# Indexer scores of the first 128 tokens: one matmul over two half-length key runs, added on the way out of PSUM

## The chip, the cores and the metric

One core of a Trainium2 chip runs the whole kernel. The metric is the device time of an execution in microseconds. The matmuls run on TensorE (PE in the profile), elementwise work on VectorE (DVE) and ScalarE (ACT), a few masks on GpSimd (POOL); SyncE (SP) issues the DMAs.

## The reference

A decoder trunk of two layers over 256 tokens of width 1024. In each layer a normed input is projected to eleven parts. Branch A is attention over the 64 keys that an indexer picks for each query; branch B is a gated linear recurrence; both are gated, merged and projected back. What the change touches is the indexer:

```
dots = einsum('bqhd,bsd->bqhs', iq, ik)          # 16 heads of 64, one key vector per position
idx_score = einsum('bqh,bqhs->bqs', iw, relu(dots))
idx_score = where(key_pos <= query_pos, idx_score, -inf)
sel = top_k(idx_score, 64)
```

Because of the causal mask, a query among the first 128 tokens needs the scores of the first 128 keys only.

## The kernel before

Activations stand transposed in SBUF, 128 features by 256 tokens. Every float32 operand of a matmul is split into a high part, rounded to the fast float32 format of TensorE (`F32R`), and a low part, the remainder; a product is the sum of three matmuls (high x high, low x high, high x low; function `mm3`). The weights stream from HBM in chunks of 128x1024 (`raw`), which ScalarE or VectorE rounds to `wh` and VectorE subtracts to `wl`; a chunk feeds 8 blocks, so 24 matmuls of 256 columns, or fewer of 512.

The program is not written in the order in which it runs. `Program` records every operation with an engine, a cost and its tiles. `issue` then plans: it takes, over all engines, the operation that can start first, and among those that can start at once the one that is due first. A TensorE operation is due at its place in the written order plus `pg.late`; `LATE_DOTS` puts the dots 40 us of matmul time later than they are written, so that they are spread between other matmuls. The other engines' operations are due when a matmul needs them or a buffer of a ring must be free again (`deadlines`). Each engine then runs its list strictly in that order. So a change of one function moves instructions in the whole program.

The indexer, class `Layer`: `head` makes the keys (`ikr`, 64x256), writes the rounded half `kh` and the rest `kl` twice, on partitions 0 to 63 and 64 to 127. `queries` turns two pairs of heads into `st`, two tiles that hold one head's high and low part one above the other on the 128 partitions, so that one matmul with `kh` gives high x high and low x high, and one with `kl` the rest. `dots` then runs for 8 pairs of heads and for `t` = 0 and 1, the first and the last 128 tokens. It takes one of two PSUM banks of the pool `pq` (which also serves the gate matmuls `gps` and the attention logits `lg`), makes four matmuls of 256 columns into it, takes the Relu on ScalarE into `rl`, and adds both heads, weighted, to the scores `wk` on VectorE. For `t` = 0 all 256 keys are multiplied, and 128 are read:

```
            for a in range(2):
                w = st[a][:, t * P:t * P + P]
                mm(ps[:, a, :], w, self.kh, True, False)
                mm(ps[:, a, :], w, self.kl, False, True)
            ...
            act(rl[:, :, :n], ps[:, :, :n], AF.Relu)
```

In the profile's rows `dots` is the bank, `iqs` are the tiles `st`, `rps` the matmuls of the recurrent branch, `mb`, `ma` and `ga` gates, `xc` the convolution, `sg` an activated gate, `g` its split product. Helpers record the operations, so their lines stand in the rows: L506 ScalarE, L513 and L515 the rounding copy on ScalarE or VectorE, L519 VectorE with two tensors, L534 and L538 VectorE with a scalar, L545 matmul, L548 transpose, L552 and L1031 DMAs.

Of the kernel before, what the change touches and what calls it, by code (L numbers as in the profile page):

```python
# [12 lines left out]
F32R = mybir.dt.float32r  # L13
I32 = mybir.dt.int32
AF = mybir.ActivationFunctionType
OP = mybir.AluOpType

P = 128
D = 1024
T = 256  # L20
# [221 lines left out]
def real(a):  # L242
    return a.ap() if isinstance(a, V) else a
# [222 lines left out]
def trunk(ctx, tc, xT, pos, pre, par, fgb, wst, out):  # L466
# [7 lines left out]
    pg = Program()  # L474
    cnt = [0]

    def nm(s):
        cnt[0] += 1
        return f"{s}{cnt[0]}"


    def const(s, shape, dt=F32, bufs=1, tag=None):
        return pg.tile(cp, tag or s, [P] + shape, dt, nm(s), bufs)
# [7 lines left out]
    def f2(s):  # L491
        return pg.tile(fp, "f2", [P, 2, T], F32, nm(s), F2)
# [4 lines left out]
    def bank(pool, s):  # L497
        return pg.tile(pp, pool, [P, 2, T], F32, nm(s), {"pp": 4, "pq": 2, "pt": 2}[pool])


    def act(o, i, func, **kw):
        c = (160 if i.psum() else 140) + 0.833 * o.size() + (200 if "accum_out" in kw else 0)
        aps = [kw[k] for k in ("scale", "bias") if isinstance(kw.get(k), V)]
        outs = [o] + ([kw["accum_out"]] if "accum_out" in kw else [])
        pg.op("act", c + 93 * len(aps), outs, [i] + aps,
              lambda: nc.scalar.activation(real(o), real(i), func, **{k: real(v) for k, v in kw.items()}),  # L506
              TABS.get(func))
# [9 lines left out]
    def tt(op, o, a, b):  # L517
        pg.op("dve", 67 + 1.046 * o.size(), [o], [a, b],
              lambda: nc.vector.tensor_tensor(real(o), real(a), real(b), op=op))  # L519
# [4 lines left out]
    def add(o, a, b):  # L524
        tt(OP.add, o, a, b)
# [4 lines left out]
    def tsc(o, a, s1, s2, op0, op1=None):  # L530
        c = 67 + 1.046 * o.size() if a.psum() else 69 + 0.52 * o.size()
        kw = {} if op1 is None else {"op1": op1}
        pg.op("dve", c, [o], [a, s1, s2],
              lambda: nc.vector.tensor_scalar(real(o), real(a), real(s1), real(s2), op0=op0, **kw))  # L534

    def stt(o, a, s, b, op0, op1):
        pg.op("dve", 129 + 1.046 * o.size(), [o], [a, s, b],
              lambda: nc.vector.scalar_tensor_tensor(real(o), real(a), real(s), real(b), op0=op0, op1=op1))  # L538
# [4 lines left out]
    def mm(o, w, m, start, stop, grp=False, cost=None):  # L543
        pg.op("pe", cost or (m.size() + 32) / 2.4, [o], [w, m],
              lambda: nc.tensor.matmul(real(o), real(w), real(m), start=start, stop=stop, skip_group_check=grp))  # L545
# [15 lines left out]
    class Stream:  # L561
        def __init__(self):
            self.pos = 0
            self.raws = {}
            self.parts = {}
            self.nload = 0
# [257 lines left out]
    class Layer:  # L824
        def __init__(self, l, xg, norm):
            self.l = l
            self.xg = xg
            self.norm = norm
            self.h = []
            self.sga, self.sma, self.smb = {}, {}, {}  # L830
            self.xc, self.xs, self.rix, self.sy, self.g = {}, {}, {}, {}, {}
            self.rope = {}
            self.aT = []
            self.m = []
            self.banks = {}
            self.wk = [const("wk0", [P]), const("wk1", [T])]
            self.kh = const("kh", [T], F32R)
            self.kl = const("kl", [T], F32R)
            self.iwq = const("iwq", [2, 16])

        def pair(self, key, i):
# [69 lines left out]
        def dots(self, i, st, t):  # L911

            pg.late = LATE_DOTS
            ps = bank("pq", "dots")
            for a in range(2):
                w = st[a][:, t * P:t * P + P]
                mm(ps[:, a, :], w, self.kh, True, False)
                mm(ps[:, a, :], w, self.kl, False, True)
            pg.late = 0.0
            n = P * (t + 1)  # L920
            o = self.wk[t]
            rl = f2("rl")
            act(rl[:, :, :n], ps[:, :, :n], AF.Relu)
            for a in range(2):
                w = self.iwq[:, t, 2 * i + a:2 * i + a + 1]
                if i == 0 and a == 0:
                    tsc(o, rl[:, a, :n], w, None, OP.mult)
                else:
                    stt(o, rl[:, a, :n], w, o, OP.mult, OP.add)
# [444 lines left out]
```

## Time and profile before

| | |
|---|---|
| median of 3 runs | 699.63 us (699.3 to 701.31) |
| the profiled execution | 699.13 us |
| its span, first to last instruction | 697.3 us |
| instructions in the span | 12505 |
| PE busy, matmuls | 686.9 us, 99%, 4684 |
| DVE busy | 601.4 us, 86%, 1177 |
| ACT busy | 480.0 us, 69%, 775 |
| POOL busy | 7.1 us, 1%, 18 |
| HBM read | 119.77 MB |

Busy times are sums over an engine's instructions; a row in the listings below gives the length of one record, and records of one engine overlap at their ends, so the distance from one start to the next is shorter than a record. The chain that ended last is the profile's way of following the end back to what it waited for.

### The profile page before, as it was taken

The page shows a single profiled execution, that of the slowest core. Times are in us where ns is not written, and L with a number is a line of the kernel's source. Part 1 is how long each engine was busy: PE and PEld are TensorE (multiplying, and loading weights), DVE is VectorE, ACT ScalarE, POOL GpSimd, SP SyncE. Part 2 cuts the span into 40 slices and gives each one's busy share as a digit, 9 for nine tenths or more (in the row PEclk, how much of TensorE's full clock was granted, in tenths as well). Part 3 has the DMA queues.
Part 4 walks back from the last instruction along what each step waited for, and adds up shares of the span by engine and source line. Part 5 has one row for each costly group of instructions (what it writes and reads, how often), then busy time and mean ns, then how long its engine had stood idle before and what let it go on. Part 6 is the DMA issues. An engine that isn't in the chain of part 4 may idle for free.

```text
span 697.3 us, 12505 instructions
## 1 busy us (share of the span) xinstructions
PE 686.9 (99%) x4684; PEld 636.6 (91%) x4684; DVE 601.4 (86%) x1177; ACT 480.0 (69%) x775; POOL 7.1 (1%) x18
## 2 busy tenths in 40 slices
PE   9999999999999999999999999999999999999996
PEld 8988999998899998888999999999999898988885
DVE  7999999999898959857779999989978987897563
ACT  7898675698996748534559766688879765664433
POOL 0000000000000000000000000000000000000000
PEclk9999999999999999999999999999999999999998
DMA  8745666776756462665553566766675655445621
GB/s 281 238 153 166 211 187 195 218 206 200 212 180 200 152 189 65 209 182 183 170 176 118 185 192 184 198 211 197 222 207 185 186 184 156 147 145 161 197 72 61
DMA packets 37697, 125.24 MB, mean 180 GB/s; under 512 B 4677, under 2 KB 6661, under 8 KB 37637
## 3 DMA queue, kind: packets, MB, share of 16 engines
q1 hardware_dynamic: 37636, 124.44, 57.9%
q8 instruction: 37, 0.61, 0.4%
q14 instruction: 24, 0.19, 0.1%
HBM read 119.77 MB, written 1.05 MB: 173 GB/s over the span
## 4 chain that ended last, share of the span: by engine, by line
PE 87%; DVE 2%; ACT 1%; DMA 0%; issue 0%
PE rps L545 15%; PE yb L545 9%; PE q L545 7%; PE k L545 7%; PE ops L545 6%; PE ya L545 6%; PE v L545 6%; PE mb L545 6%; PE ga L545 6%; PE ma L545 5%; PE gps L545 4%; PE iq L545 3%; PE dots L545 2%; PE av L545 2%; PE lg L545 2%; PE ptp L548 1%
## 5 line engine op out<-in xcount | busy, mean ns | idle before, releaser
L519 DVE TENSOR_TENSOR wl<-raw,wh 128x1024 fp32r<-128x1024 f32 x223 | 271.3, 1220 | 57.7 <-ACT wh L513 56.1
L513 ACT ACTIVATE wh<-raw 128x1024 fp32r<-128x1024 f32 x196 | 207.1, 1059 | 136.0 <-PE ya L545 22.4
L545 PE MATMUL rps<-hl,wh 128*128 128x256 f32 x352 | 99.6, 283 | 0.5 <-DVE hl L519 0.5
L545 PE MATMUL rps<-hh,wh 128*128 128x256 f32 x352 | 99.6, 283 | 0.3 <-ACT hh L513 0.3
L545 PE MATMUL rps<-hh,wl 128*128 128x256 f32 x352 | 99.5, 283 | 0.0
L545 PEld LDWEIGHTS rps<-hl,wh 128*128 128x128 f32 x352 | 67.4, 191 | 0.7 <-DVE hl L519 0.7
L545 PEld LDWEIGHTS rps<-hh,wh 128*128 128x128 f32 x352 | 67.3, 191 | 0.7 <-ACT hh L513 0.5
L545 PEld LDWEIGHTS rps<-hh,wl 128*128 128x128 f32 x352 | 67.4, 191 | 0.2
L545 PE MATMUL yb<-wh,g 128*128 128x512 f32 x176 | 59.5, 399 | 0.0
L545 PE MATMUL iq<-xg,wh 128*128 128x256 f32 x232 | 44.9, 285 | 0.0
L545 PE MATMUL ya<-wh,aT 128*128 128x512 f32 x128 | 40.9, 395 | 0.0
L545 PEld LDWEIGHTS yb<-wh,g 128*128 128x128 f32 x176 | 32.4, 188 | 5.5
L545 PEld LDWEIGHTS iq<-xg,wh 128*128 128x128 f32 x232 | 37.2, 192 | 0.0
L545 PE MATMUL ga<-hh,wh 128*128 128x256 f32 x128 | 36.3, 283 | 0.5 <-DVE iqr L519 0.5
L545 PE MATMUL q<-hl,wh 128*128 128x256 f32 x128 | 36.4, 284 | 0.0
L545 PE MATMUL q<-hh,wh 128*128 128x256 f32 x128 | 36.3, 283 | 0.0
L545 PE MATMUL k<-hh,wl 128*128 128x256 f32 x128 | 36.3, 283 | 0.0
L545 PE MATMUL k<-hh,wh 128*128 128x256 f32 x128 | 36.2, 283 | 0.0
L545 PE MATMUL ga<-hl,wh 128*128 128x256 f32 x128 | 36.2, 283 | 0.0
L545 PE MATMUL q<-hh,wl 128*128 128x256 f32 x128 | 36.2, 283 | 0.0
L545 PE MATMUL ga<-hh,wl 128*128 128x256 f32 x128 | 36.2, 283 | 0.0
L545 PE MATMUL k<-hl,wh 128*128 128x256 f32 x128 | 36.2, 283 | 0.0
(269 smaller groups left out, 1923.1 us busy)
## 6 DMA issues: line engine op xcount, KB each, us to landing
raw<-in_wst_dram SPq DMA_DIRECT2D x224, 512.0 KB
xk<-xs SPq DMA_DIRECT2D x24, 48.0 KB
out_dram<-z SPq DMA_DIRECT2D x4, 256.0 KB
xf<-xs SPq DMA_DIRECT2D x8, 80.0 KB
rah<-in_wst_dram SPq DMA_DIRECT2D x2, 256.0 KB
xr<-in_xT_dram SPq DMA_DIRECT2D x1, 512.0 KB
xf<-xs SPq DMA_DIRECT2D x4, 128.0 KB
fg<-in_fgb_dram SPq DMA_DIRECT2D x2, 256.0 KB
```

The source lines that it names most:

```text
L513: lambda: nc.scalar.activation(real(o), real(i), AF.Copy),
L519: lambda: nc.vector.tensor_tensor(real(o), real(a), real(b), op=op))
L545: lambda: nc.tensor.matmul(real(o), real(w), real(m), start=start, stop=stop, skip_group_check=grp))
L548: pg.op("pe", 70, [o], [i, ident], lambda: nc.tensor.transpose(real(o), real(i), real(ident)))
```

## The change

`kh` and `kl` become two halves of one tile `khl`, 128 x 2 x 256. For the first 128 tokens each head gets one matmul whose moving operand is the first 128 columns of both halves, one run after the other: 256 columns, high sums in the first half of the output, low sums in the second. ScalarE copies the low halves of both heads out of the bank, VectorE adds the high halves from the bank, ScalarE takes the Relu in place. For the last 128 tokens the code is what it was.

```
-            self.kh = const("kh", [T], F32R)
-            self.kl = const("kl", [T], F32R)
+            self.khl = const("khl", [2, T], F32R)
+            self.kh, self.kl = self.khl[:, 0, :], self.khl[:, 1, :]
...
             ps = bank("pq", "dots")
-            for a in range(2):
-                w = st[a][:, t * P:t * P + P]
-                mm(ps[:, a, :], w, self.kh, True, False)
-                mm(ps[:, a, :], w, self.kl, False, True)
-            pg.late = 0.0
             n = P * (t + 1)
+            rl = f2("rl")
             o = self.wk[t]
-            rl = f2("rl")
-            act(rl[:, :, :n], ps[:, :, :n], AF.Relu)
+            if t == 0:
+
+                for a in range(2):
+                    mm(ps[:, a, :], st[a][:, :P], self.khl[:, :, :P], True, True)
+                pg.late = 0.0
+                act(rl[:, :, :P], ps[:, :, P:], AF.Copy)
+                add(rl[:, :, :P], rl[:, :, :P], ps[:, :, :P])
+                act(rl[:, :, :P], rl[:, :, :P], AF.Relu)
+            else:
+                for a in range(2):
+                    w = st[a][:, t * P:t * P + P]
+                    mm(ps[:, a, :], w, self.kh, True, False)
+                    mm(ps[:, a, :], w, self.kl, False, True)
+                pg.late = 0.0
+                act(rl, ps, AF.Relu)
```

The order of the instructions, at the two places that the prediction speaks of. In layer 0 on TensorE, a group of dots for the first 128 tokens stood among the matmuls of the recurrent branch like this:

```order
L545 MATMUL dots_897<-kh_762,iqs_665 128x256
L545 MATMUL rps_835<-hl_573,wh_696 128x256
L545 MATMUL dots_897<-kl_791,iqs_665 128x256
L545 MATMUL rps_835<-hh_438,wh_735 128x256
L545 MATMUL dots_897<-kh_762,iqs_672 128x256
L545 MATMUL rps_835<-hh_438,wl_813 128x256
L545 MATMUL dots_897<-kl_791,iqs_672 128x256
```

And with the change, two such groups in the same layer with one for the last tokens:

```order
L545 MATMUL dots_891<-khl_808,iqs_536 128x256
L545 MATMUL dots_891<-khl_808,iqs_544 128x256
L545 MATMUL rps_822<-hh_463,wh_734 128x256
L545 MATMUL rps_822<-hh_463,wl_783 128x256
L545 MATMUL rps_822<-hl_530,wh_734 128x256
L545 MATMUL rps_822<-hh_477,wh_734 128x256
L545 MATMUL rps_822<-hh_477,wl_783 128x256
L545 MATMUL rps_822<-hl_546,wh_734 128x256
L545 MATMUL dots_907<-khl_808,iqs_536 128x256 x2
L545 MATMUL dots_907<-khl_808,iqs_544 128x256 x2
```

A group for the first tokens has two matmuls in place of four, both with the whole key tile, and the groups now stand in blocks between stretches of other matmuls.

In layer 1 on VectorE, before, where the keys' low half is made and the first scores (`wk`) follow:

```order
L519 TENSOR_TENSOR kl_4953<-ikr_4866,kh_4922 64x256
L519 TENSOR_TENSOR sg_4938<-sg_4938,rps_4750 128x256
L519 TENSOR_TENSOR kl_4953<-ikr_4866,kh_4922 64x256
L519 TENSOR_TENSOR ga_4907<-ga_4907,ga_4830 128x512
L519 TENSOR_TENSOR wl_4978<-raw_4815,wh_4889 128x1024
L519 TENSOR_TENSOR wl_4990<-raw_4860,wh_4945 128x1024
L538 SCALAR_TENSOR_TENSOR xc_4986<-rps_4904,prm_213,xc_4986 128x255
L519 TENSOR_TENSOR wl_5010<-raw_4914,wh_4969 128x1024
L534 TENSOR_SCALAR wk_5026<-rl_5006,iwq_4606 128x128
```

With the change, the same place:

```order
L519 TENSOR_TENSOR khl_4957<-ikr_4920,khl_4957 64x256
L519 TENSOR_TENSOR wl_4985<-raw_4859,wh_4937 128x1024
L519 TENSOR_TENSOR khl_4957<-ikr_4920,khl_4957 64x256
L538 SCALAR_TENSOR_TENSOR xc_4987<-rps_4903,prm_213,xc_4987 128x255
L519 TENSOR_TENSOR wl_5004<-raw_4889,wh_4969 128x1024
L538 SCALAR_TENSOR_TENSOR xc_4987<-rps_4903,prm_213,xc_4987 128x254
L519 TENSOR_TENSOR wl_5023<-raw_4946,wh_5000 128x1024
L519 TENSOR_TENSOR rl_5017<-rl_5017,dots_5009 128x2x128
L534 TENSOR_SCALAR wk_5044<-rl_5031,iwq_4605 128x256
```

The keys' subtractions moved behind two weight subtractions (one more stands just ahead of these rows), and the first new addition stands behind two further ones, ahead of the first score. In layer 0 the rows between the last key subtraction and the first addition are of the same kinds and number. Over the whole program the order has 16 additions more on VectorE; on ScalarE 16 Relus more; of the rounding copies, VectorE has 4 more of `g`, one more of `xs`, one less of `wh` and two less of the keys, and ScalarE the opposite; TensorE has 32 matmuls less; SP has the same 305 DMAs.

## Rows read from the trace of the kernel before

**Rows 1.** The page, its parts 1 (busy us, share of the span) and 4 (chain).

```profile
PE 686.9 (99%) x4684; PEld 636.6 (91%) x4684; DVE 601.4 (86%) x1177; ACT 480.0 (69%) x775; POOL 7.1 (1%) x18
...
PE 87%; DVE 2%; ACT 1%; DMA 0%; issue 0%
```

**Rows 2.** Waits of TensorE: releaser, us in total, times, longest; 8 lines.

```profile
PE warm L545 <- DVE hpi L555: 1.1, 1, 1.1
PE dots L545 <- ACT rl L506: 0.5, 1, 0.5
...
PE mb L545 <- DVE ga L519: 0.4, 1, 0.4
...
PE gps L545 <- DMA xf<-xs: 0.2, 1, 0.2
```

**Rows 3.** Stretches: us, then busy of PE, PEld, DVE, ACT, POOL; clock, DMA.

```profile
55.00:70.00 15.00, 14.11 (x99) 12.77 (x99) 14.87 (x29) 13.05 (x24) 0.00 (x0) 1.00 0.64 191
70.00:90.00 20.00, 20.00 (x143) 18.82 (x142) 19.91 (x43) 13.66 (x24) 0.00 (x0) 1.00 0.62 188
...
120.00:150.00 30.00, 30.00 (x231) 29.02 (x230) 28.09 (x70) 22.40 (x38) 0.87 (x2) 1.00 0.70 209
...
395.00:410.00 15.00, 15.00 (x108) 13.87 (x107) 14.94 (x30) 10.65 (x19) 0.00 (x0) 1.00 0.67 210
410.00:428.00 18.00, 18.00 (x126) 16.67 (x125) 17.73 (x38) 11.55 (x21) 0.42 (x1) 1.00 0.58 172
```

**Rows 4.** The chain that ended last: start us, us, instructions.

```profile
119.47 5.76 PE rps L545 x48
125.22 2.75 PE mb L545 x12
...
403.40 0.12 PE dots L545
```

**Rows 5.** Tile dots: instructions, record ns (min/median/max), first and last start, forms.

```profile
L545 PE MATMUL dots<-kh,iqs x64: 277/282/387, 55.3 to 426.0; 128*128 128x256 f32 x64
...
L545 PE MATMUL dots<-kl,iqs x64: 277/284/287, 57.5 to 426.4; 128*128 128x256 f32 x64
L506 ACT ACTIVATE rl<-dots x32: 363/482/604, 58.6 to 426.7; 128x256 f32<-128x256 f32 x16, 128x512 f32<-128x512 f32 x16
```

**Rows 6.** Groups by line and form: busy us, mean ns, idle time before.

```profile
L519 DVE TENSOR_TENSOR sg<-sg,rps 128x256 f32<-128x256 f32 x22 | 9.0, 414 | 0.4 <-ACT sg L506 0.4
...
L506 ACT ACTIVATE asq<-rix 128x256 f32<-128x256 f32 x22 | 8.1, 410 | 0.1
...
L506 ACT ACTIVATE rl<-dots 128x256 f32<-128x256 f32 x16 | 6.0, 377 | 4.1 <-PE dots L545 2.5 <-issue 1.1 <-DVE wk L538 0.3
L513 ACT ACTIVATE kh<-ikr 64x256 fp32r<-64x256 f32 x2 | 0.8, 409 | 0.0
...
L515 DVE CAST kh<-ikr 64x256 fp32r<-64x256 f32 x2 | 0.6, 282 | 0.0
```

**Rows 7.** VectorE in order of time, both layers: start us, us, instruction.

```profile
57.26 3.50 DVE L519 TENSOR_TENSOR wl<-raw,wh 128x1024 fp32r<-128x1024 f32 x3
...
81.42 1.65 DVE L538 SCALAR_TENSOR_TENSOR xc<-rps,prm,xc 128x255 f32<-128x255 f32 x4
...
89.89 0.76 DVE L519 TENSOR_TENSOR sg<-sg,rps 128x256 f32<-128x256 f32 x2
...
395.12 0.42 DVE L519 TENSOR_TENSOR kl<-ikr,kh 64x256 fp32r<-64x256 f32 x1
```

**Rows 8.** TensorE in order of time: start us, us, instruction [idle before, releaser].

```profile
56.52 0.50 PE L545 MATMUL mb<-wh,hh 128*128 128x512 f32 x1 [0.37 <-DVE ga L519]
...
65.59 0.39 PE L545 MATMUL dots<-kh,iqs 128*128 128x256 f32 x1 [0.53 <-ACT rl L506]
...
396.67 0.28 PE L545 MATMUL dots<-kl,iqs 128*128 128x256 f32 x1
```

## The prediction

> **What bounds the kernel now.** I read the page's shares first, then who makes TensorE wait, then the stretches. TensorE is busy in 99% of the span and carries 87% of the chain that ended last; VectorE is busy in 86% and carries 2% of it, ScalarE 69% and 1% [rows 1]. The list of what the matmuls waited for has eight lines, which add up to 4.0 us in 697.3; the longest, 1.1 us, is the start of the program, and only 0.5 us is put down to dots [rows 2]. So an instruction taken from TensorE's queue shortens the run by its own slot, as long as no new wait appears there.
>
> The stretches show where one could. The index scores are worked out at about 55 to 90 us in layer 0 and 395 to 428 us in layer 1. There VectorE has nothing left: 14.87 of 15 us, 19.91 of 20, then 14.94 of 15 and 17.73 of 18, while it is back at 28.09 of 30 by 120 to 150 us. ScalarE has room from 70 us on (13.66 of 20, then 10.65 of 15 and 11.55 of 18), and the granted clock is 1.00 throughout, the 2.4 GHz level [rows 3]. The cut falls on the engine that sets the end, and the added work lands on one that is full just there.
>
> **What is removed.** The slot of a matmul is read from the chain, as the records overlap: 48 matmuls of 256 columns take 5.76 us, 0.12 us each; 12 of 512 columns take 2.75 us, 0.229 us each; and a single dots matmul among others stands there with 0.12 us [rows 4]. There are 64 dots matmuls with kh and 64 with kl, all of 256 columns [rows 5]: 16 groups for the first 128 tokens and 16 for the others (8 pairs of heads in each of 2 layers), 4 matmuls each. The change turns 4 into 2 in the 16 groups of the first tokens, each still of 256 columns. **32 x 0.12 = 3.8 us** go, with as many weight loads, which run beside the matmuls. None of it was hidden.
>
> **What one new matmul costs.** Its moving operand is two runs of 128 columns, with 128 columns between them in SBUF; the output is one run. No matmul of this trace reads two runs, so I bound it: not under the 0.12 us of a plain one of 256 columns, since as many columns pass, and not over the 0.229 us of 512 columns, the span of the two runs with the gap between [rows 4]. I take 0.12, because the gap is skipped and the column count is the same; at the other end the gain falls to 64 x 0.12 - 32 x 0.229 = 0.35 us.
>
> The Trainium skill speaks against that choice: its page Advanced Engine Details and Errata, section PSUM Cachelines, says that any non-contiguous access pattern significantly slows down matmuls. It says this of PSUM, where this output stays contiguous, and no row here shows it for a moving operand; by it the saving would be near the 0.35 us.
>
> **What is added.** *VectorE*: 16 additions of 128x256 with one operand in PSUM. The nearest row is sg<-sg,rps, the same operation and shape with an operand in PSUM: 414 ns [rows 6], and two in a row take 0.76 us, so a slot of 0.38 [rows 7]. 16 x 0.38 = 6.1 us, 3 us a layer. *ScalarE*: the Relu out of PSUM becomes a Copy out of PSUM at the same 377 ns, and 16 Relus from SBUF to SBUF come on top; nearest is asq<-rix at 410 ns [rows 6]: 6.6 us in all, into the idle quarter or third that the stretches show. The rounded key halves move between the engines in the new order: two conversions of 282 ns leave VectorE, two more of 409 ns come to ScalarE; four g, one xs and one less wh conversion shift likewise, under 1 us a layer, and all of it hides under TensorE as long as the weights arrive in time. SP issues the same transfers, POOL the same selections. I cost the added instructions themselves at nothing: the VectorE backlog that they lengthen by 3 us a layer is worked off later, at 120 us and beyond, where VectorE idles 1.9 us in 30 [rows 3]. Should that cover be gone, a weight half is late next, and each 0.1 us of it reaches the matmuls.
>
> **What can wait.** Two things. First, both key halves are now one tile, which the first new dots matmul needs whole. Before, the last subtraction of kl began at 395.12 and took 0.42 us, and the first matmul with kl came at 396.67 [rows 7, 8]: 1.1 us in hand. Second, the bank. A dots group has one of two PSUM banks. It was free after one ScalarE instruction; for the first tokens it is free after a ScalarE copy and a VectorE addition, which stands in a full queue. In both layers the order has, between the last khl subtraction and the first addition, two xc steps and two weight subtractions. By their rows these take 1.65/4 = 0.41 and 3.50/3 = 1.17 us each [rows 7], with the addition 2 x 0.41 + 2 x 1.17 + 0.38 = 3.5 us. In layer 1 TensorE has 20 matmuls from the first dots to the one that wants that bank, 2.4 us; in layer 0 it has 26, 3.1 us. With nothing in hand the waits are 1.1 and 0.4 us; with the 1.1 us of before in hand they are none. I take the middle in layer 1 and a little under the bound in layer 0: 0.5 + 0.3 = 0.8 us. Later groups should not add much, since a TensorE that is late finds the next bank free. Queued behind a waiting addition are the weight subtractions; behind a Relu that waits for its addition, ScalarE's next weight roundings.
>
> Two waits in the present dots stretch, 0.37 us for a gate and 0.53 us for a Relu [rows 8], I leave as they are: their releasers stand in the same full queues.
>
> **Sum.** The profiled execution took 699.13 us, a span of 697.3 and 1.83 around it; the median of the three runs, 699.63, is 0.5 above. 3.8 - 0.8 = 3.0 us less gives 696.1 from the former and 696.6 from the latter. I say **696.4 us**.
>
> **Rivals.**
> *The new waits eat most of the gain.* Twice the bounds above (the 1.1 and 0.4 us once at the first bank, and as much again where the order bunches two additions behind a weight subtraction) is 3.0 us: 699.1 - 0.8 = 698.3, and up to 700 if the reshuffled order brings another wait of the size of those now seen. For it: VectorE is full; against it: in layer 1 TensorE now runs through this stretch without idling, and 6 to 12 other matmuls stand between most groups.
> *The change doesn't do what it says*: two runs cost as 512 columns. 699.1 - 0.35 + 0.8 = 699.5.
> *Slower: each addition holds TensorE.* If the bank is wanted before the addition every time, each of the 16 additions passes its 0.41 us to TensorE: 16 x 0.41 = 6.6, and 699.1 - 3.8 + 6.6 = 701.9. It decides from a wait of 0.37 us per group on, (3.8 + 2.1)/16. For it: two banks, and a release that needs two engines. Against it: now all the waits of dots for a Relu come to 0.5 us [rows 2], and the order spreads the groups. The Trainium skill, Perfetto Trace Analysis, section Optimization Strategy, has a rule for this: the same gap repeating on the engine that should be saturated can mean that there is not enough PSUM for the next tile. No repeating gap is in this trace.
>
> **How the numbers follow.** 0.3%, about 2.1 us, is what a measurement of this kernel can tell from no change: faster is below 697.5, slower above 701.7. The forecast has 0.62 and gives 694.4 (all 3.8 us, and the 0.9 us of old waits gone too) to 697.7. Eaten gain has 0.20, a quarter of it still below 697.5; the slow matmul 0.07; slower 0.11. So faster 0.66, same 0.23, slower 0.11. The range 694.3 to 700.2 holds all but the slower case and a little of the second.
>
> **What would show it.** Right: 96 dots matmuls with khl and slots of 0.12 us; 16 additions of about 0.41 us; a list of TensorE's waits that has grown by 1 us or so, with the additions or ScalarE's part in it; VectorE still full to 120 us and a little longer. Wrong: dots slots near 0.23 us; a wait of dots for rl repeated in most groups; a new line of waits for weight halves or for xf. A time above 699 us would mean that one of these is there.

## The result, and the profile after

The changed kernel takes 695.84 us (median of 4 runs, 695.58 to 695.91) against 700.03 us for the kernel before (4 runs, 699.3 to 701.31); the ratio of the runs is 0.9924, with a 95% interval of 0.9904 to 0.9945. The medians alone differ by 4.2 us, a ratio of 0.994. The profiled executions are 699.13 and 695.58 us, their spans 697.3 and 693.8 us, so 3.5 us went inside the span; the first of them was quicker than all four runs of its kernel, hence the smaller difference. The forecast was 696.4 us, in a range of 694.3 to 700.2.

The page of the changed kernel, its parts 1 and 4, for [rows 1]:

```profile
PE 683.5 (99%) x4652; PEld 633.2 (91%) x4652; DVE 604.7 (87%) x1195; ACT 482.8 (70%) x788; POOL 11.0 (2%) x18
...
PE 83%; DVE 11%; ACT 2%; issue 2%; DMA 1%; SPq 0%; DVEq 0%; ACTq 0%
```

TensorE has 4652 matmuls, 32 less than before. VectorE is 3.3 us busier and ScalarE 2.8; the span got shorter nevertheless. VectorE's share of the chain rose from 2% to 11%: on the way to the end there is now a place where TensorE waits for VectorE, and from there the chain runs back along VectorE's queue. In layer 1 that place is this (start us, us, what):

```profile
412.30 0.34 DVE rl L519
...
412.69 0.50 PE dots L545 x2
```

An addition ends, and the dots matmuls that need its bank start. TensorE idles too briefly there for the list of waits below.

The tile dots and the additions, for [rows 5], and then two pieces of the chain, for [rows 4] (start us, us, instructions):

```profile
L545 PE MATMUL dots<-khl,iqs x96: 277/281/393, 60.3 to 422.9; 128*128 128x256 f32 x96
...
L519 DVE TENSOR_TENSOR rl<-rl,dots x16: 403/412/415, 62.9 to 423.6; 128x256 f32<-128x256 f32 x16
```

```profile
62.57 0.24 PE dots L545 x2
...
72.35 0.12 PE dots L545
```

96 dots matmuls stand where 128 stood: the 32 with two runs of keys, and 64 of the last tokens, which read kh or kl alone. Two of them in a row take 0.24 us, one 0.12 us, as in the kernel before. Of the 32 matmuls over two runs, 27 have 0.116 to 0.124 us from their start to the next one; four have 0.18 to 0.22 us, and one, at the wait below, 1.07. So the gap between the two runs costs nothing, and 32 x 0.12 = 3.8 us left TensorE's queue. An addition has a record of 412 ns.

What the matmuls waited for, for [rows 2] (releaser, us in total, times, longest; 7 lines, 3.7 us in all), and the stretches, for [rows 3]:

```profile
PE warm L545 <- DVE hpi L555: 1.0, 1, 1.0
PE dots L545 <- DVE rl L519: 0.8, 1, 0.8
...
PE mb L545 <- DVE sg L519: 0.3, 1, 0.3
```

```profile
55.00:70.00 15.00, 14.68 (x101) 13.22 (x100) 14.94 (x31) 13.86 (x26) 0.00 (x0) 1.00 0.74 243
70.00:90.00 20.00, 19.95 (x145) 18.78 (x144) 19.87 (x41) 16.36 (x31) 0.00 (x0) 1.00 0.52 164
...
120.00:150.00 30.00, 30.00 (x230) 29.02 (x230) 28.93 (x87) 19.11 (x30) 2.54 (x2) 1.00 0.74 216
...
392.00:407.00 15.00, 14.21 (x100) 12.95 (x100) 14.94 (x29) 10.45 (x20) 0.00 (x0) 1.00 0.70 215
407.00:425.00 18.00, 17.88 (x123) 16.37 (x122) 17.92 (x39) 13.69 (x27) 0.00 (x0) 1.00 0.56 176
```

VectorE is as full as before between 55 and 90 us and around the dots of layer 1, and at 120 to 150 us it is busy for 28.93 instead of 28.09 us. That fits a longer backlog worked off there, but the row doesn't show whose work it is: rounding copies moved between the engines as well. By its list TensorE waits for an addition in one place, between 392 and 407 us. VectorE's and then TensorE's list in order of time show it (start us, us, instruction [idle before, releaser]):

```profile
394.82 0.42 DVE L519 TENSOR_TENSOR khl<-ikr,khl 64x256 fp32r<-64x256 f32 x1
395.27 0.48 DVE L538 SCALAR_TENSOR_TENSOR xc<-rps,prm,xc 128x255 f32<-128x255 f32 x1
395.67 1.21 DVE L519 TENSOR_TENSOR wl<-raw,wh 128x1024 fp32r<-128x1024 f32 x1
396.80 0.47 DVE L538 SCALAR_TENSOR_TENSOR xc<-rps,prm,xc 128x254 f32<-128x254 f32 x1
397.19 1.21 DVE L519 TENSOR_TENSOR wl<-raw,wh 128x1024 fp32r<-128x1024 f32 x1
398.33 0.41 DVE L519 TENSOR_TENSOR rl<-rl,dots 128x256 f32<-128x256 f32 x1
```

```profile
395.40 0.47 PE L545 MATMUL dots<-khl,iqs 128*128 128x256 f32 x2
...
397.61 0.40 PE L545 MATMUL dots<-khl,iqs 128*128 128x256 f32 x2
398.79 0.74 PE L545 MATMUL dots<-khl,iqs 128*128 128x256 f32 x4 [0.79 <-DVE rl L519]
```

These are the rows of the sum in the prediction: the last key subtraction, two convolution steps, two weight subtractions, then the first addition, 3.5 us from 395.24 to 398.74. The group of dots at 398.79 needs the bank that this addition empties and waits 0.79 us for it. That is the idle time after the record before it has ended; from start to start the two matmuls before it have 1.18 us where their slots are 0.24, so the wait costs 0.94 us. The same place in layer 0, VectorE and then TensorE:

```profile
59.43 0.42 DVE L519 TENSOR_TENSOR khl<-ikr,khl 64x256 fp32r<-64x256 f32 x1
...
62.94 0.41 DVE L519 TENSOR_TENSOR rl<-rl,dots 128x256 f32<-128x256 f32 x1
```

```profile
60.26 0.88 PE L545 MATMUL dots<-khl,iqs 128*128 128x256 f32 x6
...
63.41 0.75 PE L545 MATMUL dots<-khl,iqs 128*128 128x256 f32 x4
```

Here the addition ends at 63.35, again 3.5 us behind the last key subtraction, and the dots that need the bank come at 63.41: it is free in time.

### The profile page after: what moved, and what is told of

It is laid out like the page before. It is cut to its first block, busy times and chain, and to the rows that moved or that the text cites. A ratio compares the mean times of both kernels' runs of the same rounds, so it can differ in the third digit from the quotient of the medians.

```text
span 693.8 us, 12460 instructions
## 1 busy us (share of the span) xinstructions
PE 683.5 (99%) x4652; PEld 633.2 (91%) x4652; DVE 604.7 (87%) x1195; ACT 482.8 (70%) x788; POOL 11.0 (2%) x18
## 4 chain that ended last, share of the span: by engine, by line
PE 83%; DVE 11%; ACT 2%; issue 2%; DMA 1%; SPq 0%; DVEq 0%; ACTq 0%
PE rps L545 14%; PE yb L545 9%; PE q L545 7%; PE k L545 7%; PE ops L545 6%; PE ma L545 6%; PE ya L545 6%; PE v L545 6%; PE mb L545 5%; PE ga L545 5%; PE gps L545 4%; DVE wl L519 4%; PE lg L545 2%; PE av L545 2%; PE iq L545 1%
```

## Experiments

All are edits of a few lines; the planner makes a new order for each. "Due later" means the constant `LATE_DOTS`, which places the dots among the other matmuls.

**1. The removed slots put back.** If the gain is TensorE's slots, doubling the new matmuls takes it away, with all the new work outside TensorE left in.

```
-  mm(ps[:, a, :], st[a][:, :P], self.khl[:, :, :P], True, True)
+  mm(ps[:, a, :], st[a][:, :P], self.khl[:, :, :P], True, False)
+  mm(ps[:, a, :], st[a][:, :P], self.khl[:, :, :P], False, True)
```

> The changed kernel with each of its 32 new matmuls done twice into the same bank (the scores of the first 128 tokens are doubled, which leaves their ranking as it is). Theory, the gain is the 32 slots taken from TensorE: the slots are back, so 695.8 + 32 x 0.12 = 699.7 us, less up to 0.8 us if the wait for the bank shrinks: 698.9 to 699.8. Rival, the gain comes from the reshuffled order and from old waits that went away with it: the time stays below 697.5 us.

Measured: 702.79 us, ratio to the kernel before 1.0037 (1.0023 to 1.005). The gain is gone, as the slots would have it, but the time is 3 us above the range expected. Its waits of TensorE (6.6 us in all, against 3.7 in the changed kernel) and two places in ScalarE's list:

```profile
PE dots L545 <- ACT rl L506: 1.9, 2, 1.5
...
PE gps L545 <- DMA xf<-xs: 1.0, 1, 1.0
```

```profile
401.20 1.06 ACT L513 ACTIVATE wh<-raw 128x1024 fp32r<-128x1024 f32 x1 [1.70 <-DMA raw<-in_wst_dram]
402.16 0.58 ACT L506 ACTIVATE rl<-dots 128x512 f32<-128x512 f32 x1
```

ScalarE stands for 1.70 us before a weight rounding whose chunk has not landed, and the Relu that empties a bank is queued behind it; the matmuls wait 1.5 us for that Relu. The spans differ by 701.2 - 693.8 = 7.4 us: 3.8 of slots, 2.9 of listed waits, and 0.7 that these lists don't name. To see how much of the 2.9 is this order, the same edit was run with the dots due 44 us late.

```
-LATE_DOTS = 40000.0
+LATE_DOTS = 44000.0
```

> The changed kernel with its matmuls doubled (scores doubled, same ranking) and the dots due 44 us late: does the 702.8 us of the same edit at 40 us hold? Theory, slots plus waits of the order: TensorE's slots are those of the kernel before, and the waits differ from order to order, so 699.3 to 702.5 us, not below 699. Rival, the doubled matmuls cost more than their 3.8 us themselves: again 702.5 us or more, with the same list of waits.

Measured: 700.78 us, ratio 1.0007 (0.9997 to 1.0016), waits of 3.8 us in all. The changed kernel with the same due time (experiment 4) has a span of 694.6 us and this one 698.6: 4.0 us for 32 slots and 0.1 us of waits, so 0.12 us a slot again. The medians of the two are 4.7 us apart; the executions of either differ by 0.7 to 0.8 us among themselves, so the last tenths are not to be read. The 702.8 us were slots and an unlucky order.

**2. One tile for the keys, and nothing else.**

```
-            self.kh = const("kh", [T], F32R)
-            self.kl = const("kl", [T], F32R)
+            self.khl = const("khl", [2, T], F32R)
+            self.kh, self.kl = self.khl[:, 0, :], self.khl[:, 1, :]
```

> The kernel before with kh and kl as halves of one tile and nothing else changed: 128 dots matmuls, no additions. Theory of the slots: nothing is taken from TensorE, so the time of before, 699.3 to 700.4 us, or up to 1 us more where the first dots wait for the whole key tile. Rival of the reshuffled order: the planner moves instructions here too, and a gain of 1 us or more appears without any matmul removed.

Measured: 700.83 us, ratio 1.0011 (1.0002 to 1.002). The order moves here too, and no gain comes with it: the dots' wait for a Relu is 1.7 us, where [rows 2] has 0.5. This part of the change alone costs 0.8 us in this order.

**3. What the bank behind VectorE's queue costs.** ScalarE copies both halves out, so that the bank is free without VectorE, which then adds in SBUF.

```
-                act(rl[:, :, :P], ps[:, :, P:], AF.Copy)
-                add(rl[:, :, :P], rl[:, :, :P], ps[:, :, :P])
+                act(rl, ps, AF.Copy)
+                add(rl[:, :, :P], rl[:, :, :P], rl[:, :, P:])
```

> The changed kernel with ScalarE copying both halves out of the bank (512 columns, by its rows 594 instead of 377 ns) and VectorE adding them in SBUF, so that the bank is free without VectorE. Theory, the one new wait (0.79 us of dots for an addition) is the bank held behind VectorE's queue: it goes, ScalarE's 16 x 0.22 = 3.5 us more hide, and the time is 694.8 to 695.6 us. Rival, VectorE's load as such holds TensorE, or ScalarE becomes what holds it: 695.8 us or more, with a wait of dots for ScalarE in the list.

Measured: 694.31 us, ratio 0.9914 (0.9901 to 0.9928), 1.5 us below the changed kernel, and below the range expected. All waits of its matmuls, and the group of ScalarE's copies and Relus out of the bank (busy us, mean ns | idle before):

```profile
PE warm L545 <- DVE hpi L555: 1.1, 1, 1.1
PE rps L545 <- DVE hl L519: 0.5, 1, 0.5
PE ga L545 <- DVE iqr L519: 0.5, 1, 0.5
PE mb L545 <- DVE sg L519: 0.3, 1, 0.3
PE rps L545 <- ACT hh L513: 0.3, 1, 0.3
```

```profile
L506 ACT ACTIVATE rl<-dots 128x512 f32<-128x512 f32 x32 | 18.3, 595 | 2.3 <-PE dots L545 1.7 <-DVE iqr L519 0.4
```

No dots matmul waits for anything; ScalarE's longer copies (595 instead of 378 ns, 16 times) make no matmul wait in this order. The listed waits are 2.7 us in place of 3.7: the 0.8 us for the addition and some smaller ones. Their 1.0 us doesn't account for all of the 1.5 us; the rest is not explained; this kernel, too, has an order of its own. The opposite edit, more VectorE work on the bank, adds the high halves a second time; the scores of the first 128 tokens are then not the reference's.

```
                 add(rl[:, :, :P], rl[:, :, :P], ps[:, :, :P])
+                add(rl[:, :, :P], rl[:, :, :P], ps[:, :, :P])
```

> The changed kernel with the high halves added twice (the scores of the first 128 tokens are not the reference's), so 16 more VectorE additions of 0.38 us that hold the bank, 6.1 us more of VectorE. Theory, VectorE's work hides except where a bank is wanted at once: 696 to 697.5 us. Rival, each addition passes on to TensorE because VectorE is full there: 695.8 + 16 x 0.38 = 701.9 us.

Measured: 697.75 us, ratio 0.9969 (0.9957 to 0.998), 1.9 us above the changed kernel and 0.25 above the range expected. Its page, part 1, and its two longest waits:

```profile
PE 683.6 (98%) x4652; PEld 633.4 (91%) x4652; DVE 607.3 (87%) x1207; ACT 484.7 (70%) x789; POOL 7.6 (1%) x18
```

```profile
PE gps L545 <- DMA xk<-xs: 1.3, 1, 1.3
PE dots L545 <- DVE rl L519: 1.2, 2, 0.9
```

VectorE's rounding of weights, in the changed kernel and then in this one (busy us, mean ns | idle before):

```profile
L515 DVE CAST wh<-raw 128x1024 fp32r<-128x1024 f32 x26 | 17.9, 687 | 3.9 <-PE iq L545 1.7 <-PE ma L545 0.6 <-DMA xk<-xs 0.5
```

```profile
L515 DVE CAST wh<-raw 128x1024 fp32r<-128x1024 f32 x21 | 14.5, 689 | 5.3 <-PE ma L545 1.9 <-PE iq L545 1.7 <-PE gps L545 1.0
```

The dots wait 1.2 us for additions, 0.4 more than in the changed kernel, and a gate matmul waits 1.3 us for xk, a wait that the changed kernel has not. The edit did not bring VectorE the 6.1 us that were meant, though: the planner gave five weight roundings to ScalarE, and VectorE is busy for 607.3 instead of 604.7 us, 2.6 us more. So the case in which every addition passes on (701.9 us) is out, since 16 further additions ahead of the bank cost 1.9 us and not 6.1; how much added work a full VectorE would hide, this edit doesn't show.

**4. What the order alone is worth.** The kernel before, the changed one and the one of experiment 3, each with the dots due at another time, by the one-line edit above.

> The kernel before with the dots due 44 instead of 40 us late: the same instructions, another order. It measures what the order alone is worth. Theory of the slots: within 1 us of before, 699 to 701 us. Rival, the order is what decides: a change of 2 us or more either way.

> The changed kernel with the dots due 44 instead of 40 us late. Theory: the slots stay saved, and the waits for a bank behind VectorE's queue come and go with the order, 695 to 698 us, below the same shift of the kernel before by 2 to 4.5 us. Rival, the changed kernel had a lucky order: 699 us or above.

> The kernel in which ScalarE copies both halves out, with the dots due 44 us late. Theory, its bank no longer depends on VectorE: still no wait of dots for an addition, 693.4 to 695 us. Rival, its gain over the change was the order: the same as the changed kernel with that shift, or slower.

> The changed kernel with the dots due 36 us late, a third order of it. Theory: 695 to 698.5 us with a wait of dots for an addition in the list. Rival of the lucky order: 699 us or above.

> ScalarE copies both halves out, dots due 36 us late. Theory: no wait of dots for an addition, 693.4 to 696 us, below the changed kernel at the same setting by 0.5 to 2 us. Rival: no difference between the two, so that the bank held by VectorE is worth nothing on the mean of orders.

Medians in us, by the time by which the dots are due later:

| | 36 us | 40 us | 44 us |
|---|---|---|---|
| kernel before | not run | 700.03 | 699.34 |
| changed kernel | 696.77 | 695.84 | 696.09 |
| ScalarE copies both halves | 696.60 | 694.31 | 695.40 |

The order moves a kernel by 0.7 to 2.3 us. The changed kernel is below the kernel before by 4.2 us at 40 and by 3.25 us at 44, and its slowest order is 2.6 us below the faster of the two orders of the kernel before: the luck of an order isn't what it gained. Both other orders of the copy lie above the ranges expected for them. In all three orders of the changed kernel a dots matmul waits for an addition (0.8, 0.9 and, at 36 us, 0.7 us). At 36 us the waits of the changed kernel and of the one with both halves copied, and at 44 us those of the latter, are in part these:

```profile
PE dots L545 <- DVE rl L519: 0.7, 2, 0.4
PE dots L545 <- ACT rl L506: 0.5, 1, 0.5
...
PE dots L545 <- DVE khl L519: 0.4, 1, 0.4
```

```profile
PE dots L545 <- ACT rl L506: 0.8, 1, 0.8
PE rps L545 <- ACT mb L506: 0.6, 1, 0.6
```

```profile
PE dots L545 <- ACT rl L506: 0.7, 2, 0.4
```

Without VectorE the wait for an addition is gone, but in these two orders waits for ScalarE stand in its place. At 36 us the two kernels are 0.2 us apart, which their intervals (0.9932 to 0.9969 and 0.9924 to 0.9963) can't tell from nothing. So the copy of both halves is the fastest kernel measured, at 694.31 us, and its lead over the change is 1.5, 0.7 and 0.2 us; that it is better on every order is not shown.

**5. Slots again, in the fastest kernel.** The doubled matmuls of experiment 1 in the kernel of experiment 3.

> ScalarE copies both halves out, and the new matmuls are done twice (scores doubled, same ranking). Theory: 694.3 + 32 x 0.12 = 698.1 us, 697.3 to 699.3. Rival, the gain of this version is not in the slots: below 696.5 us.

Measured: 698.75 us, ratio 0.998 (0.997 to 0.9989). The spans are 691.4 and 696.8 us: 5.4 us, of which 3.8 are slots and 1.6 the growth of the listed waits from 2.7 to 4.3 us (1.0 of it one wait of dots for a Relu). The medians are 4.4 us apart.

**6. The same saving without an addition.** The four matmuls of the first tokens cut to the 128 keys that are read, accumulated in PSUM as before.

```
-                mm(ps[:, a, :], w, self.kh, True, False)
-                mm(ps[:, a, :], w, self.kl, False, True)
+                mm(ps[:, a, :P * (t + 1)], w, self.kh[:, :P * (t + 1)], True, False)
+                mm(ps[:, a, :P * (t + 1)], w, self.kl[:, :P * (t + 1)], False, True)
```

> The kernel before with the four matmuls of the first 128 tokens cut to the 128 keys that are read (128 columns each, kh and kl accumulated in PSUM as before, no addition outside). If a slot is the columns alone: 64 x 0.06 = 3.8 us go as in the change, and no work is added, 695 to 696.3 us. If a matmul cannot follow the last one faster than its weights are loaded, or a short one runs at a lower rate: slots of 0.11 us or more, 699 us or above.

Measured: 697.88 us, ratio 0.9964 (0.9947 to 0.9981), between the two cases. No dots matmul waits here. One group in TensorE's list in order of time, and then the second to fourth weight load (PEld) of its short matmuls:

```profile
62.33 0.28 PE L545 MATMUL rps<-hh,wl 128*128 128x256 f32 x1
62.45 0.23 PE L545 MATMUL dots<-kh,iqs 128*128 128x128 f32 x1
62.51 0.27 PE L545 MATMUL dots<-kl,iqs 128*128 128x128 f32 x1
62.62 0.28 PE L545 MATMUL dots<-kh,iqs 128*128 128x128 f32 x1
62.73 0.27 PE L545 MATMUL dots<-kl,iqs 128*128 128x128 f32 x1
62.84 0.33 PE L545 MATMUL rps<-hl,wh 128*128 128x256 f32 x1
```

```profile
62.45 0.19 PEld L545 LDWEIGHTS dots<-kl,iqs 128*128 128x128 f32 x1
62.56 0.19 PEld L545 LDWEIGHTS dots<-kh,iqs 128*128 128x128 f32 x1
62.67 0.19 PEld L545 LDWEIGHTS dots<-kl,iqs 128*128 128x128 f32 x1
```

From start to start the first short matmul takes 0.06 us, and the next three 0.11 each. It is so in the whole trace: 26 of the 27 short dots matmuls behind a long one take 0.06 us, and 36 of the 37 behind another short one 0.11. So behind a long matmul a short one takes half of a long one's slot, and behind another short one it is hardly quicker than a long one. All 64 together take 5.9 us instead of 7.7, and 1.8 us is also what the span lost, though the listed waits fell by 1.3 us too and should have shortened it further. Every matmul has its own weight load, and the change halves their number as well, which this edit does not. The rows say that the loads set the pace: they start 0.11 us apart, and the second, third and fourth matmul each start 0.06 us behind their own load. No run changes the loads alone.

## Why the prediction was right

*The slots.* 32 slots of 0.12 us were forecast, with 0.12 taken for a matmul over two runs from a range that went to 0.229. The chain shows 0.12, and putting the slots back costs 3.9 us in experiment 1 (dots 44 us late) and 3.8 in experiment 5, once the change in the listed waits is taken off; at 40 us it costs 4.5, of which 0.7 stays unexplained. The medians give 4.7 and 4.4 us for the former two, with the waits in. The rule of the Trainium skill that was weighed there (Advanced Engine Details and Errata, section PSUM Cachelines) does not carry over to a moving operand of two runs of 128 columns in SBUF: by it the kernel would have stood near 699.5 us.

*The added work.* It was costed at nothing, with VectorE's reserve at 120 us as its cover. No list of the changed kernel or of the one with doubled additions (experiment 3) names a wait for a weight half in the dots stretches, and a time 4.2 us below the kernel before leaves no room for 6 us of it. The work was also less than forecast: VectorE is busy for 3.3 us more, not 6.1. The row taken for the price has two instructions in 0.76 us, the second with its whole record of 414 ns, so they start 0.35 us apart and not 0.38; and rounding copies changed engines. That the reserve at 120 us is what took the work up is argued and not shown. Doubling the additions cost 1.9 us for 2.6 us more of VectorE, part of it through another order, with a late transfer for a gate.

*The new wait.* 0.5 us in layer 1 and 0.3 in layer 0 were put in. Layer 1 has 0.79 us by the list and 0.94 from start to start, for the reason and behind the rows that were named, within the bound of 1.1. Layer 0 has none. For what TensorE has in hand the forecast took the middle of a range in layer 1 and almost nothing in layer 0; the rows show it. The first dots start 0.16 us behind the last key subtraction in layer 1 (395.24 to 395.40) and 0.41 us behind it in layer 0 (59.85 to 60.26), and the bounds of 1.1 and 0.4 less these are 0.94 and nothing. So the mechanism held to the rows, and its size was wrong in both layers: too small in one and too large in the other. That the two add up to the 0.8 us of the forecast is luck. The wait for the whole key tile, the other one that was named, does not show in the changed kernel and shows with 0.4 us in the order of 36 us.

*The old waits.* Both were left as they are. The gate's wait stayed at 0.32 us (0.37 in [rows 8]), now for `sg` in place of `ga`; the wait for a Relu, 0.53 us, went. The sum doesn't close on these alone: all listed waits together fell from 4.0 to 3.7 us, so with the slots 4.1 us should have gone, and the span lost 3.5. The 0.6 us between are, by the starts in the trace, delays too short for the list or counted short in it, like the 0.94 us above. The forecast named as a sign of being right a list that had grown by 1 us or so. The new line for the additions is there, but the list did not grow, as other waits shrank with the new order. The forecast says 3.0 us less, and 3.5 by the spans or 4.2 by the medians were measured; how near it came is in part the order's doing, which moved the changed kernel by 0.9 us in experiment 4.

*The rivals.* That the order's luck or the waits would eat the gain was priced at 698.3 to 700 us. The changed kernel in three orders lies between 695.8 and 696.8, so the case did not come about, though experiment 1 shows an order that costs 3 us. The slower case needed 0.37 us lost per group; the list has one group in sixteen, with 0.79. What was held against it, that 6 to 12 other matmuls stand between most groups, the trace doesn't bear out: of the 30 pairs of neighbouring groups within a layer, 10 have 6 to 12 matmuls between them and 15 have 4 or fewer. That the waits stayed rare is therefore not shown to come from the spread of the groups.

## What to carry to other kernels

Where TensorE sets the time, count slots: here a matmul less was worth its start-to-start distance, even though two other engines got more work for it, one of them already full. Then look at who empties the PSUM bank: with two banks, an instruction that stands in a full queue and must run before a bank is free made the matmuls wait. Letting the engine with room empty the bank, by a longer instruction, is worth trying; here it was ahead by 1.5, 0.7 and 0.2 us on three orders. In a program whose order is planned, try a few orders before a difference of 1 or 2 us is put down to an edit.

## What the runs showed that was not expected

A matmul of 128 columns takes 0.06 us behind a long one and 0.11 behind another short one, as far apart as the weight loads beside them, so cutting columns in runs of short matmuls saved 1.8 us of span where merging matmuls saved 3.5. And a late transfer held up TensorE through an engine that was a third idle: in experiment 1 a weight rounding that waited 1.70 us for its chunk held the Relu queued behind it, and with that a bank.
